# Rotary embedding on one core: how the first pair of slabs is stored, with and without a short write to the output

## The chip, the core and the metric

The kernel runs on one core of one Trainium2 chip. The metric is the device time of one execution in microseconds (us). Three runs of the kernel before gave 161.74, 161.77 and 161.85 us, a median of 161.77 us. One further execution was taken with the hardware profiler; all durations below come from that one.

## What is computed

A rotary position embedding on a float32 tensor of batch 16, sequence 512 and 16 heads of 64 numbers. Each head's first and second half are turned by the angle of the sequence position.

```python
batch, seq, dim, num_heads = 16, 512, 1024, 16     # cos, sin: (512, 32)
x = x.reshape(batch, seq, num_heads, 64)
x1, x2 = x[..., :32], x[..., 32:]
cos, sin = cos[None, :, None, :], sin[None, :, None, :]
rotated = np.concatenate([x1 * cos - x2 * sin,
                          x1 * sin + x2 * cos], axis=-1)
```

Input and output are 33.55 MB each, and each crosses between the device memory and the core's own memory once.

## The kernel before

**Tiles.** The batch is cut into 8 slabs of two batch entries (4.19 MB each). A slab lies on 128 partitions with 8 sequence positions of 1024 numbers, 32 KB, on each. Two neighbouring slabs form a pair: in the device memory the rows of a pair's partition are 64 KB in one piece, of which the even slab is the first half and the odd slab the second. The core's memory holds three such pairs (`places`, L52), so slabs 0 to 5 can be there at once, and slabs 6 and 7 (the fourth pair) go into the place of slabs 0 and 1.

**Helpers.** `here(s, n)` (L55) is the place of `n` slabs from slab `s` on, and `there(t, s, n)` (L59) the same slabs in the input or output. `load` and `store` (L68, L72) issue one transfer on SyncE's (SP's) queue, through L65. With `EVEN` or `ODD` (L76) it covers only the even or the odd partitions: 64 rows. A transfer of both slabs of a pair has rows of 64 KB, a transfer of one slab has rows of 32 KB.

**Order of the transfers.** `keep_in_program_order` holds the order in which they are written. SP issues slab 0, slab 1, the even and then the odd partitions of slabs 2 and 3, and then slabs 4 and 5 as one transfer (L79 to L97). After that come, as the passes below end: the store of slabs 0 and 1 in two transfers (even partitions, odd partitions), the load of slabs 6 and 7 in two transfers (each waits until the store of the same partitions has landed, since it overwrites them), the store of slabs 2 and 3 in one, of slabs 4 and 5 in two, of slabs 6 and 7 in one. That is 13 transfers on SP's queue.

**ScalarE's queue** issues three small transfers at the start: the tables cos and sin (64 KB each, L89) and, at L91, a write of 128 zeros from the tile `blank` (made by VectorE at L83) to the first 512 bytes of the output. The result of slab 0 lands on the same bytes later, so the first store of the output waits for that write.

**Tables.** GpSimd turns cos and sin into bf16 (L112), eight TensorE products spread them over the 128 partitions with the signs that are needed (L119), and VectorE and ScalarE copy the two products to `tabs` (L126, L151).

**Passes.** Each slab is worked on in place (L154 to L180). ScalarE casts it to bf16 into the lower part of its own place (`cast`, L145); VectorE multiplies by the two tables and adds (L167, L170); ScalarE writes the result back as float32 (L173, through L151), and then the pair's store can be issued. ScalarE casts the next slab before it copies the present one out. Slab 0 is done in two passes of half its positions, slab 7 in three (4, 2 and 2 positions).

Of the kernel before, what the change touches and what calls it, by code (L numbers as in the profile page):

```python
# [2 lines left out]

# [4 lines left out]


@with_exitstack  # L10
def kernel(
    ctx: ExitStack,
    tc: tile.TileContext,
    x: bass.AP,
    cos: bass.AP,
    sin: bass.AP,
    num_heads: int,
    out: bass.AP,
):
    nc = tc.nc  # L20
    P = nc.NUM_PARTITIONS

    batch, seq, dim = x.shape
    nh = num_heads
    hd = dim // nh
    half = hd // 2
    bf16 = mybir.dt.bfloat16
    f32 = mybir.dt.float32

    nb = 2  # L30
    nslabs = batch // nb
    rpp = nb * seq // P
    W = rpp * dim
    TP = seq // rpp
    TW = rpp * half

    out_flat = out.rearrange("b s h d -> b s (h d)")

    singles = ctx.enter_context(tc.tile_pool(name="singles", bufs=1))
    pairs = ctx.enter_context(tc.tile_pool(name="pairs", bufs=3))  # L40
    psum = ctx.enter_context(tc.tile_pool(
        name="psum", bufs=1, space=bass.MemoryType.PSUM))


    def view(t, offset, *dims):
        return dataclasses.replace(t, offset=t.offset + offset,
                                   ap=[t.ap[0], *[list(d) for d in dims]])

    places = [pairs.tile([P, 2 * W], f32, tag="pair", name="pair") for _ in range(3)]  # L52


    def here(s, n=1):  # L55
        return view(places[s // 2 % 3], s % 2 * W, (1, n * W))


    def there(t, s, n=1):  # L59
        return bass.AP(tensor=t.tensor, offset=t.offset + s // 2 * 2 * P * W + s % 2 * W,  # L60
                       ap=[[2 * W, P], [1, n * W]])


    def issue(out, in_):
        tc.keep_in_program_order(nc.sync.dma_start(out=out, in_=in_))  # L65


    def load(s, n=1, parts=slice(None)):  # L68
        issue(here(s, n)[parts], there(x, s, n)[parts])


    def store(s, n=1, parts=slice(None)):  # L72
        issue(there(out_flat, s, n)[parts], here(s, n)[parts])


    EVEN, ODD = slice(0, P, 2), slice(1, P, 2)  # L76


    load(0)  # L79


    blank = singles.tile([1, P], f32, tag="blank")
    nc.vector.memset(blank, 0.0)  # L83


    cos_sb = singles.tile([TP, TW], f32, tag="cos_sb")
    sin_sb = singles.tile([TP, TW], f32, tag="sin_sb")
    for t, src in ((cos_sb, cos), (sin_sb, sin)):
        tc.keep_in_program_order(nc.scalar.dma_start(out=t, in_=bass.AP(  # L89
            tensor=src.tensor, offset=src.offset, ap=[[TW, TP], [1, TW]])))  # L90
    tc.keep_in_program_order(nc.scalar.dma_start(out=bass.AP(  # L91
        tensor=out_flat.tensor, offset=out_flat.offset, ap=[[P, 1], [1, P]]), in_=blank))

    load(1)
    for parts in (EVEN, ODD):
        load(2, 2, parts)
    load(4, 2)  # L97


    pick = singles.tile([TP, 4 * P], bf16, tag="pick")  # L100
    nc.gpsimd.memset(pick, 0.0)  # L101
    for h in range(2):
        for g in range(2):
            part = view(pick, (2 * h + g) * P, (TP // 2, 2 * P // TP), (1, TP // 2))
            nc.gpsimd.affine_select(  # L105
                out=part, in_=part, compare_op=mybir.AluOpType.not_equal,
                fill=1.0 - 2.0 * g, base=-h, pattern=[[0, 2 * P // TP], [-2, TP // 2]],
                channel_multiplier=1)

    tab1 = singles.tile([TP, 2 * TW], bf16, tag="tab1")  # L110
    for i, t in enumerate((cos_sb, sin_sb)):
        nc.gpsimd.tensor_copy(out=view(tab1, i * TW, (1, TW)), in_=t)  # L112

    accs, tabs = [], []
    for h in range(2):
        acc = psum.tile([P, 2 * rpp * hd], f32, tag=f"acc{h}", name="acc")
        for i in range(2):
            for f in range(2):
                nc.tensor.matmul(  # L119
                    view(acc, i * rpp * hd + f * half, (hd, rpp), (1, half)),  # L120
                    view(pick, (2 * h + i * f) * P, (1, P)),
                    view(tab1, i * TW, (half, rpp), (1, half)),
                    start=True, stop=True)
        accs.append(acc)
        tabs.append(singles.tile([P, 2 * rpp * hd], bf16, tag=f"tab{h}", name="tab"))
    nc.vector.tensor_copy(out=tabs[0], in_=accs[0])  # L126

    passes = []
    for s in range(nslabs):
        r = 0
        for n in {0: (4, 4), nslabs - 1: (4, 2, 2)}.get(s, (rpp,)):
            passes.append((s, r, n))
            r += n


    def halves(u):
        s, r, n = u  # L140
        t = here(s).bitcast(bf16)
        return [view(t, (2 * r + i * n) * dim, (1, n * dim)) for i in range(2)]


    def cast(u):  # L145
        s, r, n = u
        copy(halves(u)[0], view(here(s), r * dim, (1, n * dim)))


    def copy(out, in_):  # L150
        tc.keep_in_program_order(nc.scalar.copy(out=out, in_=in_))  # L151


    for i, u in enumerate(passes):  # L154
        s, r, n = u
        if i == 0:
            cast(u)
            cast(passes[1])
            copy(tabs[1], accs[1])
            cast(passes[2])  # L160
        elif s > 0:
            for v in passes:
                if v[0] == s + 1:
                    cast(v)
        lo, up = halves(u)
        for t, a in ((up, 0), (lo, rpp * hd)):
            nc.vector.tensor_mul(  # L167
                out=t, in0=lo,
                in1=view(tabs[s % 2], a + r * hd, (hd, n), (0, nh), (1, hd)))
        nc.vector.tensor_add(  # L170
            out=up, in0=up, in1=view(lo, half, (hd, n * nh), (-half, 2), (1, half)))

        copy(view(here(s), r * dim, (1, n * dim)), up)  # L173
        if s == 1:
            for act in (store, load):
                for parts in (EVEN, ODD):
                    act(0 if act is store else 6, 2, parts)
        elif s % 2 and r + n == rpp:
            for parts in (EVEN, ODD) if s == 5 else (slice(None),):
                store(s - 1, 2, parts)  # L180


# [1 line left out]
_INS = ['x', 'cos', 'sin', 'num_heads']  # L184
_OUTS = [((16, 512, 16, 64), 'float32')]

_NUMBERS = {'num_heads': 16}


# [26 lines left out]
```

## Time and profile before

| what | value |
|---|---|
| median of three runs | 161.77 us |
| the profiled execution's own time | 161.8 us |
| its span (first to last instruction) | 160.0 us |
| busy: ScalarE, VectorE | 114.0 us (71%), 108.0 us (68%) |
| busy: TensorE, GpSimd | 2.0 us, 2.6 us |
| moved by the DMA engines | 67.24 MB, mean 420 GB/s over the span |

The span does not cover 1.8 us of the execution's time. There are 16 DMA engines; a queue's "share" is the time of all its packets divided by sixteen times the span.

The transfers on SP's queue, from the timeline of SP and the times from issue to landing (landing = issue + that time; for the fifth, seventh, ninth and twelfth it is worked out from the chain of waits or from the median of two):

| transfer | issued at | landed at |
|---|---|---|
| load slab 0 | 0.74 | 13.5 |
| load slab 1 | 1.18 | 23.4 |
| load slabs 2, 3, even partitions | 1.65 | 33.1 |
| load slabs 2, 3, odd partitions | 2.26 | 42.75 |
| load slabs 4, 5 | 2.9 | 62.2 |
| store slabs 0, 1, even partitions | 56.80 | 72.0 |
| store slabs 0, 1, odd partitions | 57.36 | 81.9 |
| load slabs 6, 7, even partitions | 71.99 | 91.4 |
| load slabs 6, 7, odd partitions | 81.95 | 101.0 |
| store slabs 2, 3 | 84.48 | 120.4 |
| store slabs 4, 5, even partitions | 115.06 | 130.1 |
| store slabs 4, 5, odd partitions | 115.6 | 139.6 |
| store slabs 6, 7 | 137.69 | 159.2 |

They land in the order in which they were issued, and 4.19 MB lands about every 9.7 us from the first landing to the last.

### The profile page before, as it was taken

How to read it: one execution, taken by the hardware profiler on the slowest of the kernel's cores; microseconds unless marked ns; L12 is line 12 of the kernel's file. 1: busy time of each engine (PE TensorE's matmuls, PEld its weight loads, DVE VectorE, ACT ScalarE, POOL GpSimd, SP SyncE). 2: the span in 40 equal slices, each digit the busy share in tenths (PEclk: the TensorE clock that was granted, in tenths of full speed). 3: DMA queues.
4: the chain of work that ended last, by engine and by line, in shares of the span. 5: the costliest groups of instructions: out<-in, count | busy, mean ns of one | idle time of the engine just before them, and what ended most of it. 6: DMA issues, size and time to landing. Idle time of an engine off the chain costs nothing.

```text
span 160.0 us, 176 instructions
## 1 busy us (share of the span) xinstructions
PE 2.0 (1%) x8; PEld 1.0 (1%) x8; DVE 108.0 (68%) x35; ACT 114.0 (71%) x24; POOL 2.6 (2%) x11
## 2 busy tenths in 40 slices
PE   0010300000000000000000000000000000000000
PEld 0000100000000000000000000000000000000000
DVE  0000699999935998999899899919999997000000
ACT  3005959993299999999999995799999969400000
POOL 4000000000000000000000000000000000000000
DMA  7999999699699699897996996996996996996991
GB/s 262 405 401 405 393 524 524 262 524 524 262 524 524 262 524 410 377 524 344 442 524 278 508 524 278 508 524 262 524 524 262 524 491 295 524 491 295 524 459 66
DMA packets 1522, 67.24 MB, mean 420 GB/s; under 512 B 241, under 2 KB 370, under 8 KB 370
## 3 DMA queue, kind: packets, MB, share of 16 engines
q1 hardware_dynamic: 1360, 67.11, 97.7%
q10 hardware_dynamic: 162, 0.13, 0.3%
HBM read 33.69 MB, written 33.55 MB: 420 GB/s over the span
## 4 chain that ended last, share of the span: by engine, by line
DMA 53%; DVE 14%; ACT 12%; issue 5%; ACTq 2%; SPq 1%
DMA pair<-in_x_dram 37%; DMA out_dram<-pair 15%; ACT pair L151 12%; DVE pair L167 10%; DVE pair L170 4%; ACTq L211 1%; SPq L65 1%; ACTq L151 0%
## 5 line engine op out<-in xcount | busy, mean ns | idle before, releaser
L151 ACT CAST pair<-pair 128x8192 bf16<-128x8192 f32 (+5 forms) x22 | 111.8, 5153 | 20.9 <-DMA pair<-in_x_dram 19.5
L167 DVE TENSOR_TENSOR pair<-pair,tab 128x8192 bf16<-128x8192 bf16 (+2 forms) x22 | 71.4, 3259 | 9.8 <-ACT pair L151 9.4
L170 DVE TENSOR_TENSOR pair<-pair 128x8192 bf16<-128x8192 bf16 (+2 forms) x11 | 35.8, 3259 | 0.3
L126 DVE CAST tab<-acc 128x1024 bf16<-128x1024 f32 x1 | 1.2, 1225 | 16.2 <-PE acc L119 16.2
L151 ACT ACT_TABLE_LOAD x1 | 1.3, 1283 | 2.8 <-issue 2.8
L119 PE MATMUL acc<-tab,pick 64*128 64x256 bf16 x8 | 2.0, 405 | 16.0 <-POOL tab L112 16.0
L119 PEld LDWEIGHTS <-pick 64*128 64x128 bf16 x8 | 1.0, 130 | 16.5 <-issue 14.5
L105 POOL TENSOR_SCALAR_AFFINE_SELECT pick<-pick 64x128 bf16<-64x128 bf16 x4 | 1.1, 302 | 0.1
L151 ACT CAST tab<-acc 128x1024 bf16<-128x1024 f32 x1 | 1.0, 1003 | 0.0
L83 DVE MEMSET blank<- 1x128 f32 x1 | 0.2, 165 | 0.8 <-PEq L197 0.8
L112 POOL CAST tab<-cos_sb 64x256 bf16<-64x256 f32 x1 | 0.4, 389 | 8.5 <-DMA cos_sb<-in_cos_dram 8.5
L101 POOL MEMSET pick<- 64x512 bf16 x1 | 0.5, 517 | 0.3 <-POOLq L197 0.3
L112 POOL CAST tab<-sin_sb 64x256 bf16<-64x256 f32 x1 | 0.4, 394 | 4.9 <-DMA sin_sb<-in_sin_dram 4.9
L197 POOL MEMSET const-float32-0.0<- 128x1 f32 x1 | 0.1, 103 | 0.2 <-issue 0.2
L197 POOL MEMSET const-bfloat16-1.0<- 128x1 bf16 x1 | 0.1, 106 | 0.0
L197 POOL MEMSET const-uint8-127<- 128x1 uint8 x1 | 0.1, 106 | 0.0
L197 POOL MEMSET const-float32-1.0<- 128x1 f32 x1 | 0.1, 103 | 0.0
## 6 DMA issues: line engine op xcount, KB each, us to landing
pair<-in_x_dram SPq DMA_DIRECT2D x2, 4096.0 KB, 17.5
out_dram<-pair SPq DMA_DIRECT2D x6, 22.8
pair<-in_x_dram SPq DMA_DIRECT2D x5, 36.0
cos_sb<-in_cos_dram ACTq DMA_DIRECT2D x1, 64.0 KB, 10.1
sin_sb<-in_sin_dram ACTq DMA_DIRECT2D x1, 64.0 KB, 14.8
out_dram<-blank ACTq DMA_DIRECT2D x1, 0.5 KB
```

What stands on the lines that cost most here:

```text
L65: tc.keep_in_program_order(nc.sync.dma_start(out=out, in_=in_))
L83: nc.vector.memset(blank, 0.0)
L101: nc.gpsimd.memset(pick, 0.0)
L105: nc.gpsimd.affine_select(out=part, in_=part, compare_op=mybir.AluOpType.not_equal, fill=1.0 - 2.0 * g, base=-h, pattern=[[0, 2 * P // TP] ...
L112: nc.gpsimd.tensor_copy(out=view(tab1, i * TW, (1, TW)), in_=t)
L119: nc.tensor.matmul(view(acc, i * rpp * hd + f * half, (hd, rpp), (1, half)), view(pick, (2 * h + i * f) * P, (1, P)), view(tab1, i * TW, ( ...
L126: nc.vector.tensor_copy(out=tabs[0], in_=accs[0])
L151: tc.keep_in_program_order(nc.scalar.copy(out=out, in_=in_))
L167: nc.vector.tensor_mul(out=t, in0=lo, in1=view(tabs[s % 2], a + r * hd, (hd, n), (0, nh), (1, hd)))
L170: nc.vector.tensor_add(out=up, in0=up, in1=view(lo, half, (hd, n * nh), (-half, 2), (1, half)))
L197: nc = _bacc.Bacc("TRN2", target_bir_lowering=False, num_devices=1)
L211: with _tile.TileContext(nc) as tc:
```

## The change

Two things are changed. The tile `blank`, its zeroing on VectorE and its write of 512 bytes to the output on ScalarE's queue are taken out. And the first pair is stored in three transfers in place of two: once both passes of slab 0 are copied out, the even partitions of slab 0 (64 rows of 32 KB, 2.1 MB); after slab 1's copy, the even partitions of slab 1 (2.1 MB) and then the odd partitions of both (64 rows of 64 KB, 4.2 MB). The loads of slabs 6 and 7 follow as before; the one of the even partitions now waits for two stores.

```diff
-    blank = singles.tile([1, P], f32, tag="blank")
-    nc.vector.memset(blank, 0.0)
...
-    tc.keep_in_program_order(nc.scalar.dma_start(out=bass.AP(
-        tensor=out_flat.tensor, offset=out_flat.offset, ap=[[P, 1], [1, P]]), in_=blank))
...
         copy(view(here(s), r * dim, (1, n * dim)), up)
-        if s == 1:
-            for act in (store, load):
-                for parts in (EVEN, ODD):
-                    act(0 if act is store else 6, 2, parts)
+        if s == 0 and r + n == rpp:
+            store(0, 1, EVEN)
+        elif s == 1:
+            store(1, 1, EVEN)
+            store(0, 2, ODD)
+            for parts in (EVEN, ODD):
+                load(6, 2, parts)
         elif s % 2 and r + n == rpp:
             for parts in (EVEN, ODD) if s == 5 else (slice(None),):
                 store(s - 1, 2, parts)
```

In the order of the built program, nothing else moves: TensorE and GpSimd have the same instructions, VectorE the same but the zeroing, ScalarE the same but the short write. ScalarE's cast of slab 6 waits for four transfers' semaphores in place of two.

## The prediction

> **What bounds the kernel now.** I read the engines' busy times first, then the queues, then the span cut into stretches. No compute engine is near its limit. The queue of SP is:
>
> ```profile
> span 160.0 us, 176 instructions
> ...
> PE 2.0 (1%) x8; PEld 1.0 (1%) x8; DVE 108.0 (68%) x35; ACT 114.0 (71%) x24; POOL 2.6 (2%) x11
> ...
> q1 hardware_dynamic: 1360, 67.11, 97.7%
> q10 hardware_dynamic: 162, 0.13, 0.3%
> ```
>
> q1 is SP's queue, q10 ScalarE's. The packets of q1 fill 97.7% of sixteen engines' 160.0 us: 156.3 us of each engine's span, and q10 another 0.5 us. Some 3.2 us are left, and the stretches tell where (the last two columns are the DMA share and GB/s; a packet is counted where it starts, so a stretch can read over 1):
>
> ```profile
> 0.00:1.70 1.70, 0.00 (x0) 0.02 (x1) 0.17 (x1) 0.00 (x0) 1.10 (x7) 1.00 0.00 0
> 1.70:62.30 60.60, 2.02 (x8) 1.02 (x8) 40.24 (x13) 42.81 (x10) 1.49 (x5) 1.00 1.03 435
> 62.30:72.00 9.70, 0.00 (x0) 0.00 (x0) 9.17 (x3) 9.70 (x3) 0.00 (x0) 1.00 1.00 432
> ...
> 101.00:120.40 19.40, 0.00 (x0) 0.00 (x0) 15.93 (x4) 19.30 (x5) 0.00 (x0) 1.00 1.00 432
> 120.40:139.70 19.30, 0.00 (x0) 0.00 (x0) 14.69 (x10) 15.87 (x5) 0.00 (x0) 1.00 1.00 435
> ...
> 158.90:160.00 1.10, 0.00 (x0) 0.00 (x0) 0.00 (x0) 0.00 (x0) 0.00 (x0) 1.00 0.00 0
> ```
>
> 1.7 us pass before the first packet and 1.1 us after the last; the other 0.4 us is mostly that the sixteen engines do not end at the same moment (in the packet records they end between 157.8 and 158.9, an average loss of 0.5 us). Between 1.8 and 158 us the records show next to no moment with an engine idle. Loads and stores run at the same rate, 432 to 435 GB/s. So the bound is this queue: its bytes at that rate, from the first packet to the last. An earlier or later issue costs or gains nothing as long as the transfer is queued before the one ahead of it has run out.
>
> The compute engines must only keep the queue fed. Where that is tight, two lines of SP's timeline and then a piece of the chain of waits show:
>
> ```profile
> 56.80 1.16 SPq L65 DMA_DIRECT2D out_dram<-pair  x2
> ...
> 137.69 0.35 SPq L65 DMA_DIRECT2D out_dram<-pair  x1
> ```
>
> ```profile
> 81.95 19.07 DMA pair<-in_x_dram
> 101.02 0.02 issue
> 101.04 0.02 ACTq L151
> 101.06 0.04 issue
> 101.10 7.03 ACT pair L151
> ```
>
> The first line of the timeline is the store of slabs 0 and 1, issued at 56.80 while the load of slabs 4 and 5 runs until 62.2 (issue 2.9 plus 59.3 to landing): 5.4 us in hand. The second is the last store, issued at 137.69, while the one ahead lands at 139.6. From issue to first packet took about 1.0 us at the start (0.74 to 1.8), and landing is some 0.4 us after a transfer's last packet, so the first packet of the last store can go at about 138.7 and the queue runs dry at about 139.2: some 0.5 us in hand. Both sides of this margin start at the landing of slab 7's odd partitions at 101.02: ScalarE idles there (2.81 us before 101.10, released by that DMA) and starts with it, and the 38.6 us of stores ahead of the last one are queued behind the same load. A shift of that landing therefore moves both, and the margin stays.
>
> **The change part by part.**
>
> *Early store of slab 0's even partitions.* ScalarE's timeline has three operations from 23.42 that take 14.03 us together (the cast of slab 1 and slab 0's two copies), so the store can be issued at 37.5. The queue has then 24.7 us of loads ahead of it (to 62.2). Transfers land in the order of issue throughout the table above, so its packets go when the even store's packets went before, from about 62 us on. Worth: 0. If it ran ahead instead, slabs 4 and 5 would land 4.8 us later (2.1 MB at 435 GB/s), at 67; ScalarE reaches slab 4's cast at 70.8 (slab 1's copy ends at 56.78, then the cast of slab 3 and the copy of slab 2, 7.02 us each), so that is hidden as well. No other instruction of SP stands between the two stores; its wait from 37.5 to 56.8 holds up nothing.
>
> *Slab 1's even and the pair's odd partitions.* Issued at 56.8 and, one issue of 0.52 us later, 57.4, still 4.8 us before the queue is dry. The additional issue (0.35 to 0.6 us in SP's rows) lies at 37.5, behind nothing.
>
> *Rows of 32 KB in place of 64 KB for 4.19 MB.* Each engine moves 8 packets of 32 KB where it moved 4 of 64 KB. Packet records: most 64 KB packets take 2.418 us, undisturbed 32 KB packets (late in slab 1's load) 1.213 to 1.219. That is 8 x 1.216 - 4 x 2.418 = +0.06 us, paid in full, since the queue is the bound. No store of 32 KB rows is in the trace. Lower bound 0. Upper bound: slab 1's load of 32 KB rows landed 9.9 us after slab 0's (13.5 to 23.4), and 4.19 MB of 64 KB rows 9.6 to 9.7 after the one ahead (91.4 to 101.02, 33.1 to 42.75): +0.2 us, although sin's packets ran there too. I take 0.06, as the packets are the nearest row.
>
> *One more transfer on the queue.* Between neighbouring transfers no gap shows: the 38.6 us from 101.0 to 139.6 hold three stores of 16.78 MB in all, 434.7 GB/s, the rate within a transfer. So 0 to 0.02 us. [...]
>
> *The load of slab 6's even partitions* now waits for two stores. The later one, slab 1's even, lands at 72.0 + 0.06; the load is then issued 10 us before the queue is dry (81.9). Worth 0; if that cover were gone, its issue to first packet, 1.0 us.
>
> *The short write.* VectorE's zeroing (0.17 us at 0.8) and ScalarE's issue (0.79 us at 1.96) go; ScalarE has nothing to do until slab 0 lands at 13.5, so both were hidden. On the DMA engines it was one packet of 27 ns on one engine. SP waited for it until 18.2, far before 56.8. Worth 0 to -0.03 us. That its absence costs is the first rival.
>
> *ScalarE's cast of slab 6* has one more semaphore wait; a wait with its issue takes 0.06 us in the chain above (101.04 to 101.10). It falls in the 0.5 us margin: 0 now, 0.06 if the margin were gone.
>
> Sum: 161.8 (profiled execution; the median is 161.77) + 0.06 + 0.01 - 0.02 = 161.85 us.
>
> **Rivals.**
>
> *The first real write now pays what the short one paid* (slower). If writes to the output start slowly once, the 16 engines pay at 62 us, with the queue full behind them. Nearest row: the first packet of each engine at the start took 1.47 to 2.04 us against 1.21, with the next ones 0.6 us per engine in all. For it: the last load packets before the first store already take 2.43 to 2.76 in place of 2.418, 0.17 us per engine, while at the later turn to stores (near 99 us) it is 0.06. Against: the short write ran on one engine, so the other fifteen met their first write at 62 us before as well. And the short write's own packet took 27 ns, and its landing (18.2) came 0.5 us after its last packet, as with other transfers. Price 0.1 to 0.6 us beside the sum; from 0.25 on it is a slower kernel: 162.4 us.
>
> *The early store smooths the turn* (faster). With a store queued 25 us ahead, the 0.17 us at the turn from loads to stores could go, and the engines, which end up to 1.1 us apart, could end closer; half of the 0.5 us loss there is 0.25. Together 161.4 us. Against: before, the store was also queued 5 us ahead, two packets per engine.
>
> *The last store comes late*: if slab 7's chain is lengthened by over the 0.5 us in hand, the excess counts fully. Only the 0.06 us wait speaks for it. 162.0 to 162.3 us.
>
> *One transfer more is paid in full* (slower): if the queue stood still between the two even stores from the end of the one to the start of the next, the price would be the 1.0 us from issue to first packet and the 0.4 us from last packet to landing, 163.3 us. Against: no such gap between any other two.
>
> **How the numbers follow.** Within 0.2% (0.32 us) is about what a measurement of this kernel can tell from no change: from 161.45 to 162.09. The forecast has 0.50 and lies there. First write: 0.32, of which 0.04 is too small to show. Smoother turn: 0.13. Late last store: 0.03, two thirds of it slower; one transfer in full: 0.02. Slower: 0.28 + 0.02 + 0.02 and 0.01 for a full price of the 32 KB rows together with a little else, 0.33; faster 0.13 and 0.02 for gains I don't see, 0.15; within, the remaining 0.52. The range goes from 161.4 (turn and ends) to 162.5 (first write with the upper bound of the rows' price, 161.8 + 0.6 + 0.1).
>
> **What would show it.** Right: the first store issued near 37.5 and landing near 67 behind the load at 62.2; slab 1's even near 72.0, the odd store near 82.0, slab 7's odd partitions at 101.1; the last store issued at 137.8 with the one ahead landing after 139.5; q1's time 0.04% of the span higher. The first-write rival: packets of the first store well over 1.22 us, and every landing from 67 on late by the same amount. The smooth turn: the last packets of slabs 4 and 5 at 2.418. The late last store: DMA idle near 139. Wrong altogether: the early store's packets amid the loads, or a stretch after 62 us whose share falls below 1.

## The result, and the profile after

The changed kernel takes 189.08 us (median of four runs, 188.99 to 189.12) against 161.81 us: a ratio of 1.1686, with a 95% interval from 1.1671 to 1.1701. It is 27.3 us slower; 161.85 us was forecast, with a range from 161.4 to 162.5. The profiled execution took 189.1 us, its span is 187.3 us in place of 160.0.

The page of the changed kernel gives the busy times, the DMA share in 40 slices, and the queues:

```profile
span 187.3 us, 176 instructions
...
PE 2.0 (1%) x8; PEld 1.0 (1%) x8; DVE 108.0 (58%) x34; ACT 114.0 (61%) x24; POOL 2.6 (1%) x11
...
DMA  6999999998999900001999999959999998659995
...
q1 hardware_dynamic: 1440, 67.11, 84.7%
q10 hardware_dynamic: 160, 0.13, 0.2%
```

No engine does more work, and the bytes are the same. SP's queue, at 97.7% before, is at 84.7%, and the slices show the hole: four of 4.7 us each without any DMA. Cut into stretches (after the stretch the busy time of TensorE, its weight loads, VectorE, ScalarE and GpSimd, then the granted clock, the DMA share and GB/s):

```profile
1.80:62.20 60.40, 2.02 (x8) 0.92 (x7) 27.10 (x10) 30.35 (x8) 1.38 (x5) 1.00 1.00 424
62.20:66.60 4.40, 0.00 (x0) 0.00 (x0) 0.88 (x1) 0.00 (x0) 0.00 (x0) 1.00 0.83 357
66.60:88.80 22.20, 0.00 (x0) 0.00 (x0) 13.28 (x3) 8.09 (x2) 0.00 (x0) 1.00 0.00 0
88.80:125.60 36.80, 0.00 (x0) 0.00 (x0) 29.79 (x7) 36.80 (x6) 0.00 (x0) 1.00 1.05 427
```

For 22.2 us, from 66.6 to 88.8, no packet starts: in the packet records the last one ends at 66.9 and the next starts at 88.9, some 1.1 us after the next store is issued. The chain of waits has the way into that hole and out of it (start, duration, what):

```profile
33.72 3.61 ACT pair L145
37.33 0.02 issue
37.34 29.84 DMA out_dram<-pair
67.19 0.03 issue
67.22 0.02 DVEq L161
67.24 0.04 issue
67.28 4.44 DVE pair L161
...
80.66 0.02 ACTq L145
```

Slab 0's last copy ends at 37.33, and the early store is issued at once. It lands 29.84 us later, behind the loads. Only then does VectorE begin a pass of three operations: that of slab 1. The timeline of the engines over this time (start, duration, operation; in brackets the idle time before it and what ended it) shows who stands behind:

```profile
49.74 8.88 DVE L161 TENSOR_TENSOR pair<-pair,tab 128x8192 bf16<-128x8192 bf16 x2 [17.77 <-ACT pair L145]
58.65 4.42 DVE L164 TENSOR_TENSOR pair<-pair 128x8192 bf16<-128x8192 bf16 x1
67.28 8.88 DVE L161 TENSOR_TENSOR pair<-pair,tab 128x8192 bf16<-128x8192 bf16 x2 [4.21 <-DMA out_dram<-pair]
76.20 4.43 DVE L164 TENSOR_TENSOR pair<-pair 128x8192 bf16<-128x8192 bf16 x1
80.72 20.86 ACT L145 CAST pair<-pair 128x8192 f32<-128x8192 bf16 x3 [31.01 <-DVE pair L164]
87.76 1.14 SPq L65 DMA_DIRECT2D out_dram<-pair  x2
```

In the kernel before, the timeline has slab 1's pass at 32.0, and slab 2's behind it at 49.9:

```profile
32.02 8.88 DVE L167 TENSOR_TENSOR pair<-pair,tab 128x8192 bf16<-128x8192 bf16 x2
40.94 4.42 DVE L170 TENSOR_TENSOR pair<-pair 128x8192 bf16<-128x8192 bf16 x1
```

Now VectorE does slab 2 first, at 49.7, and starts slab 1 at 67.28, released by the landing of the store (DMA out_dram<-pair). ScalarE stands idle for 31.0 us, since its next operation in order is the copy of slab 1. The other stores of the pair are issued at 87.76 in place of 56.8, when the queue has been dry for 21 us.

The built program says the same: the first VectorE operation on slab 1 waits for the semaphore of the early store (the counter that tells of its landing). The pass overwrites slab 1's half of the pair's tile, while the store reads the other half, so the data need no such wait. The framework sets it: it takes the store of every second partition of slab 0 and the bf16 view of slab 1 as overlapping. The runs below change the store and the tile, and with them the wait goes; that the bf16 view has a part in it no run shows by itself.

The 27.3 us add up so, from the packet records and as a mean over the sixteen engines: 22.4 us without a packet around the hole, 2.7 us more near 164 (the last store is issued late, at 165.75), and 2.0 us of slow packets near 101 and 121. That is 27.1 us; the prediction's 0.06 us for the 32 KB rows comes on top.

### The profile page after: what moved, and what is told of

It reads as the page before. It is cut to its first block, busy times and chain, and to the rows that moved or that the text cites. A ratio compares the mean times of both kernels' runs of the same rounds, so it can differ in the third digit from the quotient of the medians.

```text
span 187.3 us, 176 instructions
## 1 busy us (share of the span) xinstructions
PE 2.0 (1%) x8; PEld 1.0 (1%) x8; DVE 108.0 (58%) x34; ACT 114.0 (61%) x24; POOL 2.6 (1%) x11
## 3 DMA queue, kind: packets, MB, share of 16 engines
q1 hardware_dynamic: 1440, 67.11, 84.7%
## 4 chain that ended last, share of the span: by engine, by line
ACT 33%; DMA 28%; DVE 21%; issue 5%; ACTq 1%; SPq 0%; DVEq 0%
ACT pair L145 33%; DMA out_dram<-pair 16%; DVE pair L161 14%; DMA pair<-in_x_dram 12%; DVE pair L164 7%; ACTq L208 1%; SPq L65 0%; ACTq L145 0%; DVEq L161 0%
## 5 line engine op out<-in xcount | busy, mean ns | idle before, releaser
L161 DVE TENSOR_TENSOR pair<-pair,tab 128x8192 bf16<-128x8192 bf16 (+2 forms) x22 | 71.4, 3259 | 37.9 <-ACT pair L145 33.3
L164 DVE TENSOR_TENSOR pair<-pair 128x8192 bf16<-128x8192 bf16 (+2 forms) x11 | 35.8, 3259 | 0.3
```

What stands on the lines that cost most here:

```text
L161: nc.vector.tensor_mul(out=t, in0=lo, in1=view(tabs[s % 2], a + r * hd, (hd, n), (0, nh), (1, hd)))
L164: nc.vector.tensor_add(out=up, in0=up, in1=view(lo, half, (hd, n * nh), (-half, 2), (1, half)))
```

## Experiments

Each ratio is to runs of the kernel before, taken beside the experiment on the same chip, with its 95% interval in brackets.

**Store late.** The three stores as in the change, but none before slab 1's pass.

```diff
-        if s == 0 and r + n == rpp:
-            store(0, 1, EVEN)
-        elif s == 1:
+        if s == 1:
+            store(0, 1, EVEN)
             store(1, 1, EVEN)
```

> The three stores of the first pair as in the changed kernel (slab 0's even partitions, slab 1's even ones, the pair's odd ones), but slab 0's is issued behind slab 1's copy-out, so that no pass of slab 1 comes after it in program order; no short write. Theory (the cost is VectorE's pass on slab 1 waiting until slab 0's early store has landed): VectorE starts slab 1 at about 32.0 us, no DMA idle between 67 and 88 us, 161.9 us, of which 0.06 for the 32 KB rows. Rival (the three transfers themselves, with their 32 KB rows at a 128 KB pitch, or the missing short write cost it): about 189 us.

Measured: 161.92 us, ratio 1.0008 (0.9996 to 1.0020). VectorE no longer waits for any store; its waits in this run are

```profile
DVE tab L120 <- PE acc L113: 17.1, 1, 17.1
DVE pair L161 <- ACT pair L145: 9.8, 5, 4.5
```

The three transfers, their 32 KB rows and the missing short write cost nothing that can be told from zero. The store was not issued behind slab 1's copy-out, as expected, but at 45.34, when VectorE's pass on slab 1 had ended. SP's list of waits and its timeline show that the same overlap is now a wait of the store for the pass:

```profile
SPq L65 <- DVE pair L164: 41.8, 1, 41.8
```

```profile
45.34 12.49 SPq L65 DMA_DIRECT2D out_dram<-pair  x3
```

**A tile for each slab.** The early store stays, the shared tile goes.

```diff
+    slabs = [singles.tile([P, W], f32, tag=f"slab{i}", name="slab") for i in range(2)]
...
+        if s // 2 % 3 == 0:
+            return view(slabs[s % 2], 0, (1, W))
...
+        if n == 2 and s // 2 % 3 == 0:
+            return [store(s + i, 1, parts) for i in range(2)]
```

> The changed kernel with its early store of slab 0's even partitions, but slabs 0 and 1 (later 6 and 7) have a tile each in place of one for the pair, so that the store and slab 1's pass share no tile. All transfers of these four slabs then have 32 KB rows, 18 transfers on SP's queue from first to last or so. Theory (the wait on the shared tile is the whole cost): store issued at 37.4 us and landing near 67.2 as in the changed kernel, VectorE on slab 1 at 32.0 us all the same, 162.1 us (161.8 plus four times 0.06 for 16.8 MB more in 32 KB rows). Rival (a write queued early among the loads is itself what costs): 185 us or more.

Measured: 162.07 us, ratio 1.0023 (1.0013 to 1.0032). The store is issued as early as in the changed kernel, and slab 1's pass does not wait (timeline):

```profile
32.14 8.88 DVE L168 TENSOR_TENSOR slab<-slab,tab 128x8192 bf16<-128x8192 bf16 x2
37.60 21.09 SPq L68 DMA_DIRECT2D out_dram<-slab  x4
41.05 4.42 DVE L171 TENSOR_TENSOR slab<-slab 128x8192 bf16<-128x8192 bf16 x1
42.94 7.02 ACT L152 CAST pair<-pair 128x8192 bf16<-128x8192 f32 x1 [5.37 <-DMA pair<-in_x_dram]
49.87 7.01 ACT L152 CAST slab<-slab 128x8192 f32<-128x8192 bf16 x1
```

It lands after 29.5 us, at 67.1, as in the changed kernel. So the early write does no harm; the wait for it does. The expectation counted 16.8 MB more in 32 KB rows; the stores of slabs 0, 1, 6 and 7 and the loads of slabs 6 and 7 are 25.2 MB, which by its own price makes 162.1 as well (161.77 + 6 x 0.06).

**The short write alone**, out of the kernel before and back into the changed one (the diff of the change's first part, and its reverse).

> The kernel before with the short write to the output and its tile taken out, nothing else. Theory (the wait is the whole cost): 161.8 us, within 0.1 of the kernel before. Rival (the first real write pays what the short one paid): 162.2 to 162.5 us, with slow first packets of the first store near 62 us.

> The changed kernel with the short write to the output put back. Theory (the wait is the whole cost): 189.1 us, VectorE's wait for the early store as in the changed kernel until about 67.2 us. Rival (the missing short write has a share in the 27 us): clearly below 189, down to 162 if it is all of it.

Measured: 161.87 us, ratio 1.0002 (0.9991 to 1.0013), and 189.41 us, ratio 1.1710 (1.1692 to 1.1727). Taken out alone, the short write changes nothing that can be told from zero; put back, it takes nothing off the 27 us, and VectorE's wait stays:

```profile
67.45 4.43 DVE L168 TENSOR_TENSOR pair<-pair,tab 128x8192 bf16<-128x8192 bf16 x1 [3.79 <-DMA out_dram<-pair]
```

The rival of a first write that pays once is out: it asked for 162.2 us or more in the first of the two runs.

**VectorE in program order**, with the wait in place (the three operations of L161 and L164 under `keep_in_program_order`).

> The changed kernel with VectorE's passes kept in program order (slab 1 before slab 2; the changed kernel's scheduler had put slab 2 first). The wait for slab 0's early store stays. Theory A (the wait until the store lands at 67.2 sets slab 1's pass, the changed order only fills the wait): 189.1 us, slab 1 at 67.2 to 80.6, slab 2 behind it. Theory B (the changed order itself is what costs): well below 189.

Measured: 189.10 us, ratio 1.1683 (1.1653 to 1.1713). VectorE idles until the store has landed and then does slab 1:

```profile
67.44 8.89 DVE L161 TENSOR_TENSOR pair<-pair,tab 128x8192 bf16<-128x8192 bf16 x2 [35.20 <-DMA out_dram<-pair]
```

35.2 us is the wait's full length. That the scheduler put slab 2 first hid most of it from the table of waits (4.2 us there), and cost nothing.

**The store's landing moved to 48 us**: the load of slabs 4 and 5 goes behind it, once in the scheduler's order and once in program order.

```diff
-    load(4, 2)
...
             store(0, 1, EVEN)
+            load(4, 2)
```

> The changed kernel with the load of slabs 4 and 5 issued behind the early store of slab 0's even partitions, so that this store lands at about 47.7 us (behind the load of slabs 2 and 3, 42.7, plus 4.9) in place of 67.2. VectorE's order has slab 2 mostly ahead of slab 1, as in the changed kernel. Theory A (VectorE then is the limit: slab 2 from 49.7, slab 1 done by 76.4 and copied by 83.4, in place of 80.6 and 87.7): 4.2 us less than the changed kernel, 184.9 us. If the time to the store's landing counted alone: about 170 us.

> The same with VectorE's passes kept in program order. Theory A: slab 1 waits until 47.7 in place of 67.2 (without a wait it starts at 32.0), is done at 61.0 and copied at 68.1; DMA idle only from about 67 to 69 and some 3 us twice later, where slabs 4 to 7 come late from ScalarE and VectorE; last store issued near 147: 170.5 us. If the loss didn't follow the store's landing: near 185.

Measured: 184.92 us, ratio 1.1424 (1.1397 to 1.1452), and 170.02 us, ratio 1.0504 (1.0478 to 1.0530). In the second the wait and what follows are

```profile
48.12 8.88 DVE L160 TENSOR_TENSOR pair<-pair,tab 128x8192 bf16<-128x8192 bf16 x2 [15.90 <-DMA out_dram<-pair]
57.04 4.42 DVE L163 TENSOR_TENSOR pair<-pair 128x8192 bf16<-128x8192 bf16 x1
61.38 8.88 DVE L160 TENSOR_TENSOR pair<-pair,tab 128x8192 bf16<-128x8192 bf16 x2
61.55 20.86 ACT L144 CAST pair<-pair 128x8192 f32<-128x8192 bf16 x3 [11.39 <-DVE pair L163]
68.60 1.14 SPq L65 DMA_DIRECT2D out_dram<-pair  x2
```

The time follows the end of slab 1's pass: at 80.6 it is 189.1, at 76.4 184.9, at 61.5 170.0, and in the kernel before, where it ends at 45.4, the queue covers it. Here the order does matter: once the store lands (at 48.0) before slab 2 is cast (at 50.1), VectorE's turn for slab 2 is what keeps slab 1 waiting, and program order is 14.9 us faster.

**Adjacent partitions.** The changed kernel with partitions 0 to 63 and 64 to 127 for slabs 0, 1, 6 and 7.

```diff
+    LOW, HIGH = slice(0, P // 2), slice(P // 2, P)
...
-            store(0, 1, EVEN)
+            store(0, 1, LOW)
```

> The changed kernel with the first place's stores and reloads split into partitions 0 to 63 and 64 to 127 in place of even and odd ones: the same sizes, number and order of transfers, the same early store at 37.4. With adjacent partitions the framework sees that the early store and slab 1's pass do not touch, and the built program has no wait between them. Theory (the wait is the whole cost): VectorE on slab 1 at 32.0 us, and 161.9 us if 64 adjacent partitions are moved as fast as 64 alternate ones (25.2 MB are moved so; the trace has no row for it). Rival (the early store costs by itself): 185 us or more.

Measured: 200.25 us, ratio 1.2390 (1.2339 to 1.2441). The expected 161.9 us missed, for a reason apart from the wait. The wait is gone, and VectorE does slab 1 at 33.3 us (timeline, then stretches of DMA):

```profile
33.34 8.88 DVE L162 TENSOR_TENSOR pair<-pair,tab 128x8192 bf16<-128x8192 bf16 x2
37.59 20.45 SPq L65 DMA_DIRECT2D out_dram<-pair  x3
```

```profile
100.00:110.00 10.00, 0.00 (x0) 0.00 (x0) 4.82 (x2) 0.00 (x0) 0.00 (x0) 1.00 1.05 216
140.00:150.00 10.00, 0.00 (x0) 0.00 (x0) 4.36 (x1) 10.00 (x2) 0.00 (x0) 1.00 1.06 459
```

The queue does not run empty (over the stretches from 40 to 160 us the mean DMA share is 0.99), but while the halves are moved it runs at half its rate. The 16.8 MB moved so (the expectation said 25.2, which is wrong) take 76.3 us by the landings, from 62.2 to 138.5, or 220 GB/s; in the kernel before they took 38.8 us (62.2 to 101.0), or 432 GB/s. That is 37.5 us more, and the profiled execution, at 199.05 us, is 37.3 us above the one before. So this run shows that without the wait slab 1 isn't late, but its time can't speak of the rest. It also shows what alternate partitions are worth here: 432 GB/s against 220. What sets the lower rate no run shows.

**By slabs in place of partitions**: slab 0 and slab 1 stored whole, slabs 6 and 7 loaded one by one.

```diff
         if s == 0 and r + n == rpp:
-            store(0, 1, EVEN)
+            store(0, 1)
         elif s == 1:
-            store(1, 1, EVEN)
-            store(0, 2, ODD)
-            for parts in (EVEN, ODD):
-                load(6, 2, parts)
+            store(1, 1)
+            for v in (6, 7):
+                load(v)
```

> What the change was after, cut by slabs in place of partitions: slab 0 is stored whole (128 rows of 32 KB) once copied out, slab 1 whole later, and slabs 6 and 7 are loaded one by one, each waiting for the store of its own slab; no short write. The built program has no wait of slab 1's pass for the early store. Theory (the queue is the bound, and an early store is worth nothing without the wait): four transfers of 4.2 MB in 32 KB rows, +0.24 us by the packets, 162.0 us; slab 6 lands at 91.4 and is cast at 98.3 in place of 101.1, so the last store is issued some 2.8 us earlier, at 135, for which the queue gives nothing. Rival (an early store smooths the turn to stores, or the earlier last store gains): 161.4 or less.

Measured: 161.74 us, ratio 1.0009 (0.9995 to 1.0023). The first store is issued 19 us earlier than in the kernel before (56.80), and slab 1's pass does not wait for it (timelines of VectorE and of SP):

```profile
32.15 8.88 DVE L161 TENSOR_TENSOR pair<-pair,tab 128x8192 bf16<-128x8192 bf16 x2
```

```profile
37.61 19.65 SPq L65 DMA_DIRECT2D out_dram<-pair  x2
```

The last store is issued at 134.9 in place of 137.7, and the time is the same: with the wait gone, no gain shows from the early store or from the earlier end of the compute chain. The 0.24 us that its rows should cost lie inside the interval, so a gain of that size could hide behind them.

**Early against late, without the wait**: a tile for each slab, on the same chip.

> The run with a tile for each slab, but slab 0's even partitions stored behind slab 1's copy-out (issue near 56.8 in place of 37.6); nothing else moves. Theory (a transfer's issue is worth nothing as long as the queue has work): the same as with the early store, 162.1 us, within 0.15. Rival (the early issue gains or loses on its own): a difference of more than 0.3 us.

> The run with a tile for each slab and the early store once more, beside the late one on the same chip: 162.1 us, equal to the late one within 0.15.

Measured: 162.05 us late, ratio 1.0020 (1.0008 to 1.0031), and 162.11 us early, ratio 1.0026 (1.0014 to 1.0038). But this pair does not test the time of issue. SP's timeline has the first store at 37.81 in the run called late and at 37.35 in the other:

```profile
37.81 21.07 SPq L68 DMA_DIRECT2D out_dram<-slab  x4
```

```profile
37.35 21.10 SPq L68 DMA_DIRECT2D out_dram<-slab  x4
```

With a tile for each slab the store waits for slab 0's copies alone, and whatever stands ahead of it on SP's queue has been issued by then, so moving it down in the program leaves its issue where it was. The two runs show how well the time repeats (within 0.1 us). What an issue 19 us earlier is worth rests on the slabwise run against the kernel before.

No run beats the kernel before; the slabwise version equals it.

## Why the prediction was wrong

**What bounds the kernel: right.** The queue is the bound as long as it is fed: 97.7% of sixteen engines' span before. Runs that feed it differently without a gap lie between 161.7 and 162.1 us, but for the one with adjacent partitions, whose transfers run at half the rate (220 GB/s against 432).

**The step that failed** is the first of the parts, *Early store of slab 0's even partitions*, "Worth: 0", with "No other instruction of SP stands between the two stores; its wait from 37.5 to 56.8 holds up nothing." I looked for who waits behind the store on SP's queue, and at ScalarE's waits, and not for who waits for the store to land. In these runs a write to what the framework takes for a store's bytes starts only when the store has landed: here 0.1 us after the landing at 67.2, and with VectorE in program order after 35.2 us of idling. Slab 1's pass is done in place in the same tile, comes next in program order, and was made to wait: from 32.0, when it could have begun, to 67.2. The 24.7 us of loads ahead of the store, which I counted as proof that nothing changes, are most of the 29.8 us from its issue to its landing. The term put at 0 is the 27.3 us. The prediction's own sign of being wrong altogether came true: a stretch after 62 us whose DMA share falls below 1, to 0.00.

**The same omission in the text on the change.** "Nothing else moves" was wrong: in the built program VectorE's pass on slab 2 stands ahead of that on slab 1. Two passes of the same shape look alike in a list of shapes; the tiles' names and VectorE's waits show it.

**What the store itself does: right.** Issued at 37.34 (37.5 forecast), landing at 67.2 (near 67). What was to follow, slab 1's even partitions near 72, came at 94.4.

**The prices of the parts: right in size.** The sum without the wait was 161.85; the late store measured 161.92. The price of 32 KB rows, 0.06 us for 4.2 MB, gives 0.36 for the six times as much of the tiles for each slab, and 0.3 to 0.4 was measured (162.07 against 161.77, 162.05 and 162.11 against 161.73).

**One more transfer: right at next to nothing.** With a tile for each slab SP has 18 transfers in place of 13, for that same 0.3 to 0.4 us in all, which the rows' price alone makes up. Five more, each paid in full at the rival's 1.4 us (1.0 from issue to first packet, 0.4 from last packet to landing, both from the profile before), would be 7 us, an estimate from those two times; the run shows none of it on a queue that has work (mean DMA share 0.97 from 60 to 90 us).

**The rivals.** The first write: out, by the two runs with the short write alone. The smoother turn: no gain in the slabwise run, and in the changed kernel the last load packets before the first store took 2.79 us in the mean, 0.37 us per engine too long, where the kernel before lost 0.17. The late last store has a part in it (2.7 us near 164), but as a consequence. None of the rivals was the wait, though the margin I worked out, that slab 1's stores must be queued by 62 us, was the number to hold against slab 1's delay.

## What to carry to other kernels

A store that is moved ahead of work on the same tile can become a wait for that work, and the wait lasts until the store lands, not until it is issued: here behind 24.7 us of loads that were already queued. Before such a move, read in the built program the waits of every engine that writes the tile afterwards, with the tiles' names. If the framework takes disjoint parts for overlapping (here every second partition of one slab against the bf16 view of its neighbour), cut along another line, use a tile for each part, or issue behind the work. Look in the trace whether an edit moved the issue at all: a later place in the program need not mean a later issue. And where the queue is the bound, ask first whether an earlier issue can bring anything.

## What the runs showed beside that

Slow packets at two turns. In the changed kernel, with the short write kept and with VectorE in order, the sixteen 64 KB packets that start near 101 us took 3.1 us in the mean and those near 121 us 3.5 to 3.8, in place of 2.418; by the landings they are the last of the odd store and of the last load, where the queue turns from stores to loads and back. In the packet records of the two runs with the store's landing moved the same shows at their turns (3.1 us near 97 and near 82, 3.4 near 117 and 3.7 near 102), even the one whose queue stood empty for only 2.8 us. In the kernel before, the same turns cost 0 to 0.06 us. After the hole the sixteen engines run in step: those near 101 start within 0.14 us of one another, where a round in the kernel before is spread over 0.6. But the slower ones near 121 are spread over 0.5 again, so running in step is not enough to explain them. The cause stays open.

The other is the rate of 64 adjacent partitions: 220 GB/s against 432 for 64 alternate ones, for the same 16.8 MB.
